# Decoder layer on one core: a seven-product matrix scheme with three accumulators, another order of outputs, residual by token halves

## The chip, the core and the metric

The kernel runs on one core of one Trainium2 chip. The metric is the device time of one execution in microseconds (us). Before the change three runs gave a median of 2959.45 us (2957.71 to 2963.02).

## What is computed

One layer of a hybrid decoder for a prompt of 2048 tokens of width 1024 and a sample group of 8 rows. All products are float32 and carried out to nearly float32 precision. Cut to what matters:

```
h = rmsnorm(x, g_pre);  proj = h @ w_in            # 1024 x 10248
q, k: short causal conv and SiLU;  v, o, z_a, u, v_b, z_b, gate_a, gate_b
branch A: mLSTM (4 heads x 256, chunks of 128), head norm, * sigmoid(o) * silu(z_a), @ w_pa
branch B: u * (tril(W_s) layernorm(v_b) + b) * silu(z_b), @ w_pb
merged = sigmoid(gate_a) * A + sigmoid(gate_b) * B
x = x + rmsnorm(merged @ w_out, g_post)
x = x + sigmoid(x @ w_ple_gate) * rmsnorm(p @ w_ple, g_ple)
```

The sample rows go through the same layer with a stored state for each row and head (`state_C`, 256 x 256), which is read, scaled, updated, used and written back.

## The kernel before

The prompt is worked through in four passes `p` of 512 tokens. In pass 1 (`SP`) the 8 sample rows ride along: four columns more in each token half (260 in place of 256), and their own small steps. A pass is a list of 28 units (`PASS`, L53): `v`, `qk`, `og`, `gg` for each of four heads, then `ub` 0 to 3, then `pa`, `pb`, `wo` and `wg`, two of each. A unit multiplies a 1024 x 512 piece of weights with 512 tokens. It is done as a 2 x 2 block product with seven block products in place of eight (the Winograd form of Strassen's scheme): weights A11 to A22 with the sums S1 to S4, tokens B11 to B22 with the sums T1 to T4. Outputs are named (i, l): i is the column block of the weights, l the token half. `ORDER` (L58) lists the products with their accumulators in PSUM; `LATE` (L60) is another order for the unit `wo 0`, whose tokens come out of the unit `pb 1` just before it.

A block product is 24 matmuls: four slices of the contraction, two output blocks, and three terms each, because every operand is split into a high and a low part (`whi`, `wlo` for weights, `rhi`, `rlo` for tokens). ScalarE (ACT) makes the high part (`copy`, L124) and VectorE (DVE) the low part (`sub_hi`, L129); in pass 0 each fourth weight split has its low part on GpSimd (POOL). `Stream` feeds the weights: it loads some five to seven products ahead into 13 buffers. In pass 0 it also makes the sums S1 to S4 on DVE (L136, L139) and stores them, with S1, S2 and S4 already split (`CUT_KEPT`, L63). The stores and loads all go through one queue, issued by SyncE (SP, lines L117 and L120).

`run_unit` runs the products. After some of them ACT copies an accumulator to SBUF (`snap`: tiles `s` and `u`), and DVE adds such a copy to another accumulator when an output is finished and handed to `consumer`. Before the change: `a` takes A11, S2, S3 and A22, `b` takes A12, `c` takes S1, `d` takes S4. `s` is `a` after A11, `u` is `a` after S2. After S1 DVE adds `c` to `u` in place (L139, tile `u<-acc,u`); that sum completes (0,1). After S3 a second copy `u` of `a` completes (1,1) together with `c`. The outputs come in the order (0,0), (1,1), (0,1), (1,0), and (1,0) needs no add. PSUM has eight banks, shared with all small products (`acc` and `smp`); an accumulator takes one, in most units of pass 1 two.

Smaller work is written as generators: `qa`, `qb` and `qc` hold them, and `pump` in `run_unit` advances them by one step at set places between the matmuls, `drain` finishes a queue. `ahead` is a generator that is advanced once after each product. The order that the engines see is set by a planner at compile time: it goes by the order of the program and by its own estimate of when operands and buffers are free. Buffers come from pools: `t2` (`tmp`, ten), `t1` (`tiny`, eight), `p4` (`piece`, ten).

Around the change:
- `sample_head(h)` is queued on `qb` one head late (L1055, L1058). It loads two rows' state and `vb` (`load_state`), scales and updates them (`update_state`, L1116) and multiplies them (L1180).
- `b_norm` queues `sample_b` on `qc` and drains `qc` at once; `sample_b` normalises the sample's `xs` (L1229, L1230) and transposes it (L405).
- `merge` runs `pa` and `pb`. `ready` cuts the merged tokens into B11, B22, T1 to T4 and B21 for `wo`, partly between the products of `pb 1`, partly (`ready(True)`) between those of `wo 0`.
- `out_phase` runs `wo 0` and `wo 1`, scales the output by `g_post` (L1529, L1534), and takes the row scale `ors` from the sums of squares (`rms_tail`). Then the steps of `ple` (p @ w_ple in four column blocks, L1477, scaled by a `gple` loaded in the step, L1481) alternate with `residual(kh, l)`, which loads `xr` and does x + scale * output (L1549), and `turn`, which transposes the result (L1557) into `xblk`. `cut` and `sub` make B11 to T4 of the unit `wg 0` from it.

## Time and profile before

| | |
|---|---|
| runs | 2957.71, 2959.45, 2963.02 us |
| profiled execution, own time | 2958.16 us |
| its span, first to last instruction | 2956.4 us |
| mean granted TensorE clock | 0.966 |
| instructions | 56209 |
| moved by DMA | 770.38 MB, mean 261 GB/s |

PE is TensorE, DVE is VectorE, ACT is ScalarE, POOL is GpSimd, SP is the queue that issues the DMAs. L124 is a line of the kernel; helpers such as `copy` have one line for all their uses, so the tile names (out<-in) tell the uses apart, without buffer numbers. Times of an event are us from the start of the span. A matmul's end is modelled, so it is the starts that show the pace. The clock is a share of 2.4 GHz: 1.00 or 0.50.

### The profile page before, as it was taken

The numbers are of one execution on the slowest core, as the hardware profiler recorded it, in microseconds if no ns is written. First come the engines' busy times: TensorE is split into PE (matmuls) and PEld (weight loads), VectorE is DVE, ScalarE is ACT, GpSimd is POOL, SyncE is SP. The second block draws the span as 40 slices with busy tenths as digits, with TensorE's granted clock in tenths as the row PEclk, the third lists the DMA queues.
The fourth block names the chain that finished last, engine by engine and source line by source line (L and its number), as shares of the span: only waits on it lengthen the run. The fifth ranks groups of instructions, "written<-read, shape, count | busy, mean of one in ns | idle before, by whom it ended". The sixth has DMA issues, their size and how long they took to land. (4 is left out here: it accounts for less than half of the span.)

```text
span 2956.4 us, 56209 instructions
## 1 busy us (share of the span) xinstructions
PE 2724.2 (92%) x21835; PEld 2652.2 (90%) x21835; DVE 2216.6 (75%) x3641; ACT 1569.1 (53%) x2704; POOL 480.3 (16%) x549
## 2 busy tenths in 40 slices
PE   6999899787799999998988999999998999999897
PEld 6898889787789998888988999999998999999897
DVE  7898988788787766767768766765778766765776
ACT  4655656444646645544456555554456555554454
POOL 3333333223220001001012100001021100001010
PEclk9999999898899999999999999999999999999999
DMA  5566657775686887868867877778887877788886
GB/s 213 211 244 258 240 222 263 269 271 217 234 289 232 276 266 258 288 224 309 316 210 245 280 254 257 255 269 292 319 282 258 282 257 260 255 271 282 301 292 202
DMA packets 268628, 770.38 MB, mean 261 GB/s; under 512 B 30065, under 2 KB 89337, under 8 KB 268354
## 3 DMA queue, kind: packets, MB, share of 16 engines
q1 hardware_dynamic: 268362, 766.79, 74.3%
q8 instruction: 172, 2.82, 0.4%
q14 instruction: 94, 0.77, 0.1%
HBM read 595.29 MB, written 171.53 MB: 259 GB/s over the span
## 5 line engine op out<-in xcount | busy, mean ns | idle before, releaser
L487 PE MATMUL acc<-rhi,wlo 128*128 128x256 f32 (+1 forms) x4480 | 1276.9, 286 | 59.5 <-DVE wlo L129 46.6
L487 PE MATMUL acc<-rhi,whi 128*128 128x256 f32 (+1 forms) x4480 | 1291.7, 289 | 38.4 <-ACT whi L124 24.6
L487 PE MATMUL acc<-rlo,whi 128*128 128x256 f32 (+1 forms) x4480 | 1276.1, 285 | 0.0
L487 PEld LDWEIGHTS acc<-rhi,wlo 128*128 128x128 f32 x4480 | 859.9, 193 | 70.3 <-DVE wlo L129 55.5
L487 PEld LDWEIGHTS acc<-rhi,whi 128*128 128x128 f32 x4480 | 861.3, 192 | 51.1 <-ACT whi L124 28.8
L487 PEld LDWEIGHTS acc<-rlo,whi 128*128 128x128 f32 x4480 | 860.9, 192 | 0.4 <-issue 0.4
L129 DVE TENSOR_TENSOR wlo<-wraw,whi 128x1024 fp32r<-128x1024 f32 (+1 forms) x461 | 590.8, 1286 | 168.8 <-PE acc L487 66.3
L124 ACT ACTIVATE whi<-wraw 128x1024 fp32r<-128x1024 f32 (+1 forms) x503 | 527.3, 1053 | 295.5 <-PE acc L487 88.8
L484 PE MATMUL acc<-whi,rhi 128*128 128x256 f32 (+1 forms) x1792 | 518.9, 291 | 19.4 <-ACT rhi L124 7.1
L484 PE MATMUL acc<-wlo,rhi 128*128 128x256 f32 (+1 forms) x1792 | 512.1, 288 | 13.8 <-DVE wlo L129 11.8
L484 PE MATMUL acc<-whi,rlo 128*128 128x256 f32 (+1 forms) x1792 | 512.1, 287 | 7.6 <-DVE rlo L129 7.6
L484 PEld LDWEIGHTS acc<-whi,rhi 128*128 128x128 f32 x1792 | 347.7, 194 | 25.7 <-ACT whi L124 8.5
L484 PEld LDWEIGHTS acc<-wlo,rhi 128*128 128x128 f32 x1792 | 345.9, 194 | 16.9 <-DVE wlo L129 14.2
L484 PEld LDWEIGHTS acc<-whi,rlo 128*128 128x128 f32 x1792 | 347.5, 194 | 8.5 <-DVE rlo L129 8.3
L124 ACT ACTIVATE u<-acc 128x512 f32<-128x512 f32 (+1 forms) x272 | 140.7, 520 | 354.3 <-PE acc L487 287.9
L129 POOL TENSOR_TENSOR wlo<-wraw,whi 128x512 fp32r<-128x512 f32 x84 | 146.0, 1758 | 227.8 <-ACT whi L124 203.4
L139 DVE TENSOR_TENSOR u<-acc,u 128x512 f32<-128x512 f32 (+1 forms) x136 | 80.4, 592 | 80.5 <-PE acc L487 52.6
L124 ACT ACTIVATE s<-acc 128x512 f32<-128x512 f32 (+1 forms) x136 | 70.1, 518 | 99.7 <-PE acc L487 77.1
L786 POOL TENSOR_TENSOR so<-so,sz 128x512 f32<-128x512 f32 (+1 forms) x32 | 45.9, 1433 | 317.5 <-DVE sz L783 314.9
L1281 POOL TENSOR_TENSOR yb<-yb,ub 128x512 f32<-128x512 f32 (+1 forms) x32 | 46.5, 1459 | 296.4 <-DVE ub L1279 95.7
L241 POOL TENSOR_SCALAR aab<-au 128x2 f32<-128x2 f32 x32 | 7.7, 239 | 509.5 <-DVE au L879 508.5
L865 DVE SCALAR_TENSOR_TENSOR cext<-cext,fst,smp 128x258 f32<-128x258 f32 x128 | 60.3, 477 | 37.7 <-PE smp L802 37.5
(367 smaller groups left out, 3972.4 us busy)
## 6 DMA issues: line engine op xcount, KB each, us to landing
wraw<-in_w_main SPq DMA_DIRECT2D x351, 512.0 KB
xh<-xh SPq DMA_DIRECT2D x32, 512.0 KB
sg<-sgm SPq DMA_DIRECT2D x24, 512.0 KB
gsig<-sg SPq DMA_DIRECT2D x24, 512.0 KB
x<-in_x_prompt SPq DMA_DIRECT2D x16, 512.0 KB
ya<-ya SPq DMA_DIRECT2D x32, 256.0 KB
pg<-pg SPq DMA_DIRECT2D x32, 256.0 KB
xr<-in_x_prompt SPq DMA_DIRECT2D x32, 256.0 KB
```

What stands on the lines that cost most here:

```text
L124: S.activation(out, in_, AF.Copy)
L129: eng.tensor_tensor(lo, full, hi.bitcast(F32), op=ALU.subtract)
L139: (eng or V).tensor_tensor(out, a, b, op=ALU.add)
L241: G.tensor_scalar(out, ms, EPS, None, op0=ALU.add)
L484: T.matmul(outs[s], x[:, kt, s * P:(s + 1) * P], wt[:, kt, :], start=first, stop=last, skip_group_check=not opens)
L487: T.matmul(outs[s], wt[:, kt, s * P:(s + 1) * P], x[:, kt, :], start=first, stop=last, skip_group_check=not opens)
L786: G.tensor_tensor(so[:, s], so[:, s], sz[:, s], op=ALU.mult)
L865: V.scalar_tensor_tensor(cext[:, h, kt, :], cext[:, h, kt, :], gt.fst[:, h, self.c:self.c + 1], p3, op0=ALU.mult, op1=ALU.add)
L1281: G.tensor_tensor(y[:, :, l, :], y[:, :, l, :], ub[:, :, l, :], op=ALU.mult)
```

## The change

- `ORDER` becomes A11 (a), A12 (b), S2 (a), S3 (c), S1 (a), A22 (c), S4 (a): three accumulators. `u` after S2 is kept as it is, `u` after S3 is a copy of `c`. (1,1) is `a` after S1 plus the copy of S3, (1,0) is `c` after A22 plus the copy of S2, (0,1) is `a` after S4 with no add. So there are three adds per unit, and the outputs come as (0,0), (1,1), (1,0), (0,1).
- `LATE` becomes A11, S3, S2, A12, S1, A22, S4. The sums of its weights are made one product earlier, and A12 isn't loaded early any more. The order in which T1, T3, T4 and B22 are cut follows.
- In `pb` the column blocks of the weights and the token halves are swapped, so that (1,1) of the merged tokens is finished first, and (1,0) last, as before.
- The sample's state is loaded after the product of the two rows before, three steps ahead of its scaling; updates, convolution and normalisation get more steps between them; `sample_head(h)` is queued with its own head, and `sample_b` isn't drained at once.
- In `out_phase` the row scale is made by token halves, the first half within `wo 1`; `gple` (all four) and the `xr` of token half 0 are loaded during `wo 1`, those of half 1 right after a residual step has freed the buffers; residual, turn and cut follow by token halves.

```diff
-    UNITS["pb", _j] = ("w_pb", 256 * _j, 512 + 256 * _j)
+    UNITS["pb", _j] = ("w_pb", 512 + 256 * _j, 256 * _j)
...
-ORDER = [("A11", "B11", "a", True), ("A12", "B21", "b", True), ("S2", "T2", "a", False), ("S1", "T1", "c", True),
-         ("S3", "T3", "a", False), ("S4", "B22", "d", True), ("A22", "T4", "a", False)]
-LATE = [ORDER[i] for i in (0, 5, 2, 3, 4, 1, 6)]
+ORDER = [("A11", "B11", "a", True), ("A12", "B21", "b", True), ("S2", "T2", "a", False), ("S3", "T3", "c", True),
+         ("S1", "T1", "a", False), ("A22", "T4", "c", False), ("S4", "B22", "a", False)]
+LATE = [ORDER[i] for i in (0, 3, 2, 1, 4, 5, 6)]
...
-            first = "S4" if order(u) is LATE else "S2"
+            first = "S3" if order(u) is LATE else "S2"
...
         sub(b12, b22, b12)
+        cut("T3", b12)
+        yield
+        sub(b21, b21, t2)
         cut("T1", b11)
         yield
-        sub(b21, b21, t2)
-        cut("T3", b12)
+        cut("T4", b21)
         yield
         cut("B22", b22)
-        yield
-        cut("T4", b21)
         yield
...
             elif wn == "S2":
                 u2 = snap("u2", "a")
+            elif wn == "S3":
+                u3 = snap("u3", "c")
             elif wn == "S1":
-                for sel, ps in accs["c"][1]:
-                    add(u2[:, sel, :], ps, u2[:, sel, :])
-                x2 = u2
-            elif wn == "S3":
-                u3 = snap("u3", "a")
-                consumer(1, 1, Out(accs["c"][1], u3, w))
+                consumer(1, 1, Out(accs["a"][1], u3, w))
             elif wn == "A22":
-                consumer(1, 0, Out(accs["a"][1], None, w))
+                consumer(1, 0, Out(accs["c"][1], u2, w))
                 if so is not None:
                     consumer("sample", sos, None)
-            if x2 and "d" in accs:
-                consumer(0, 1, Out(accs["d"][1], x2, w))
-                x2 = None
+            else:
+                consumer(0, 1, Out(accs["a"][1], None, w))
...
-            if p == SP and h:
-                qb.append(sample_head(h - 1, st, A.gt, A.yad))
+            if p == SP:
+                qb.append(sample_head(h, st, A.gt, A.yad))
             gg_unit(A, h)
-        if p == SP:
-            qb.append(sample_head(H - 1, st, A.gt, A.yad))
...
-        update_state(0)
+        yield
+        yield from update_state(0)
         yield from rest(3)
         hps = smp([NS, DH])
         for i in range(4):
-            if i + 1 < 4:
-                load_state(i + 1)
             for b in range(2):
...
             if i < 3:
-                yield
-                update_state(i + 1)
+                load_state(i + 1)
                 yield from rest(3)
+                yield from update_state(i + 1)
+                yield from rest(2)
...
             qc.append(sample_b(A.xs, st, mv, rs, A.sm))
-            drain(qc)
...
-            run_unit(p, ("pa", j), ra, False, done, ahead=from_dram(rb, A.ybd) if j else None)
+            run_unit(p, ("pa", j), ra, False, done, ahead=from_dram(rb, [d[::-1] for d in A.ybd]) if j else None)
...
             yield
+            cut("B22", at(0, 1, 1), 0)
+            yield
+            cut("B22", at(1, 1, 1), 1)
+            yield
             cut("B11", at(0, 0, 0), 0)
             yield
             cut("B11", at(1, 0, 0), 1)
-            yield
-            cut("B22", at(0, 1, 1), 0)
-            yield
             subs(0)
-            cut("B22", at(1, 1, 1), 1)
             yield
             cuts(0)
             subs(1)
...
             def done(i, l, o):
+                i, l = 1 - i, 1 - l
                 m, g = ma[j][i][:, :, l, :], sg[i][:, :, l, :]
...
+        def fetch_x(kh, l):
+            for nq in (2 * kh, 2 * kh + 1):
+                x = xrs[nq, l] = tmp([P, 2, 256], "xr")
+                load(x, rows_of("x_prompt", 256 * nq)[:, 2 * l:2 * l + 2, :])
+
+        def fetch_ahead():
+            yield
+            for n in range(4):
+                gams.append(tiny([P, 256], "gple"))
+                load(gams[n], I["g_ple"][0, 256 * n:256 * n + 256].partition_broadcast(P))
+            yield
+            yield
+            fetch_x(0, 0)
+            yield
+            yield
+            fetch_x(1, 0)
...
+                if d == 1 and (i, l) == (1, 0):
+                    rms_part(ss, rs, 0, 2)
+
+            run_unit(p, ("wo", d), rm, True, done, slhs, fetch_ahead() if d else late)
         drain(qc)
-        rms_tail(ss, rs, n)
+        rms_part(ss, rs, 2, NC)
...
         next(embed)
         next(embed)
+        residual(0, 0)
+        fetch_x(0, 1)
+        next(embed)
+        residual(1, 0)
+        fetch_x(1, 1)
+        turn(0, 0)
+        cut("B11", xblk[0, 0])
...
         next(embed)
+        turn(1, 0)
+        residual(0, 1)
+        cut("B21", xblk[1, 0])
...
         next(embed, None)
+        residual(1, 1)
+        turn(0, 1)
...
         sub(xblk[0, 1], xblk[1, 1], xblk[0, 1])
-        cut("T1", xblk[0, 0])
+        cut("T3", xblk[0, 1])
         rms_tail(ss2, rs2, n)
         sub(xblk[1, 0], xblk[1, 0], t2)
-        cut("T3", xblk[0, 1])
+        cut("T1", xblk[0, 0])
+        cut("T4", xblk[1, 0])
         cut("B22", xblk[1, 1])
-        cut("T4", xblk[1, 0])
```

## Rows read from the trace of the kernel before

**Rows 1.** The page's first part: busy us, share of the span, instructions.

```profile
PE 2724.2 (92%) x21835; PEld 2652.2 (90%) x21835; DVE 2216.6 (75%) x3641; ACT 1569.1 (53%) x2704; POOL 480.3 (16%) x549
```

**Rows 2.** Stretches: length, busy (instructions) by engine, clock, DMA share, GB/s.

```profile
2421.30:2462.00 40.70, 40.70 (x346) 40.70 (x345) 29.89 (x45) 25.89 (x40) 2.68 (x4) 1.00 0.75 258
...
742.00:791.10 49.10, 32.73 (x227) 30.81 (x226) 36.27 (x48) 27.24 (x71) 11.65 (x10) 0.79 0.73 250
1526.10:1578.50 52.40, 37.91 (x278) 36.30 (x277) 35.66 (x66) 28.32 (x84) 8.71 (x12) 0.84 0.59 188
2205.20:2249.00 43.80, 33.40 (x227) 31.18 (x225) 29.22 (x42) 23.96 (x65) 7.10 (x8) 0.84 0.75 244
2879.50:2918.80 39.30, 30.53 (x226) 28.17 (x225) 26.54 (x40) 21.43 (x60) 6.90 (x6) 0.91 0.74 239
...
907.60:1384.80 477.20, 453.36 (x3587) 423.16 (x3586) 325.13 (x755) 248.12 (x471) 43.85 (x86) 0.99 0.79 264
1683.30:2077.60 394.30, 390.48 (x3283) 389.25 (x3282) 257.18 (x445) 211.74 (x358) 31.59 (x65) 1.00 0.78 267
...
18.20:575.20 557.00, 492.17 (x3842) 479.54 (x3841) 484.69 (x666) 310.02 (x471) 178.07 (x152) 0.94 0.65 240
1619.30:2077.60 458.30, 453.29 (x3807) 451.31 (x3806) 312.17 (x558) 247.79 (x410) 43.90 (x73) 1.00 0.78 267
...
683.70:723.80 40.10, 29.81 (x194) 28.75 (x193) 29.75 (x40) 20.09 (x37) 13.68 (x7) 0.83 0.47 170
...
2217.20:2220.60 3.40, 3.31 (x16) 3.11 (x16) 1.52 (x4) 0.00 (x0) 0.00 (x0) 0.50 0.90 295
```

**Rows 3.** Waits of PE over the span: us in total, times, longest.

```profile
PE smp L1557 <- DVE xq L1549: 32.2, 14, 9.5
...
PE smp L1180 <- DVE cs L1116: 12.8, 7, 6.1
...
PE acc L487 <- ACT u L124: 10.0, 14, 2.0
...
PE smp L405 <- DVE xos L1573: 8.0, 2, 5.1
```

**Rows 4.** DVE in order of time, tail of pass 2: start, us, what.

```profile
2214.32 1.29 DVE L1481 TENSOR_TENSOR pg<-acc,gple 128x512 f32<-128x512 f32 x2 [3.19 <-DMA gple<-in_g_ple]
...
2220.01 0.88 DVE L1549 SCALAR_TENSOR_TENSOR xq<-xq,ors,xr 128x256 f32<-128x256 f32 x2 [1.88 <-DMA xr<-in_x_prompt]
...
2240.90 1.22 DVE L136 TENSOR_TENSOR xblk<-xblk,t 128x1024 f32<-128x1024 f32 x1
2242.03 1.22 DVE L129 TENSOR_TENSOR rlo<-t,rhi 128x1024 fp32r<-128x1024 f32 x1
```

**Rows 5.** SP's issues in order of time, tail of pass 2.

```profile
2211.63 0.43 SPq L117 DMA_DIRECT2D xr<-in_x_prompt  x1
```

**Rows 6.** PE in order of time, tail of pass 2.

```profile
2217.29 1.08 PE L1557 MATMUL smp<-ident,xq 128*128 128x128 f32 x4 [3.30 <-DVE xq L1549]
```

**Rows 7.** DVE in order of time, pass 1, behind the unit `gg 3`.

```profile
1254.80 1.67 DVE L1116 SCALAR_TENSOR_TENSOR cs<-vb,kd,cs 128x256 f32<-128x256 f32 x4 [4.28 <-DMA vb<-svd]
```

**Rows 8.** The add of the product S1, in groups of DVE: busy, mean ns, idle before.

```profile
L139 DVE TENSOR_TENSOR u<-acc,u 128x512 f32<-128x512 f32 (+1 forms) x136 | 80.4, 592 | 80.5 <-PE acc L487 52.6 <-PE acc L484 20.8 <-ACT rhi L124 4.2
```

**Rows 9.** DVE in order of time, pass 2, from `pb 1` to `wo 0`.

```profile
2165.82 0.68 DVE L139 TENSOR_TENSOR mt<-acc,u 128x512 f32<-128x512 f32 x1
...
2173.04 0.68 DVE L129 TENSOR_TENSOR rlo<-t,rhi 128x512 fp32r<-128x512 f32 x1
2173.64 2.49 DVE L129 TENSOR_TENSOR rlo<-gsig,rhi 128x512 fp32r<-128x512 f32 x4
```

**Rows 10.** ACT in order of time: `pb 1` of pass 2, `og 1` of pass 3.

```profile
2161.09 0.60 ACT L124 ACTIVATE u<-acc 128x512 f32<-128x512 f32 x1 [1.76 <-PE acc L487]
...
2435.79 0.60 ACT L124 ACTIVATE u<-acc 128x512 f32<-128x512 f32 x1 [1.67 <-PE acc L487]
```

**Rows 11.** DVE in order of time, `og 1` of pass 3.

```profile
2436.88 0.68 DVE L139 TENSOR_TENSOR sz<-acc,u 128x512 f32<-128x512 f32 x1
```

More of the change, by code (lines that the diff above doesn't have):

```diff
@@ L284, in load @@
             else:
-                late = order(u) is LATE
-                for m in {"A11": ("A11", "A21", "A22") + ("A12",) * late, "A12": ("A12",) * (not late)}.get(n, ()):
+                for m in {"A11": ("A11", "A21", "A22"), "A12": ("A12",)}.get(n, ()):
                     self.fetch((p, u, m), given(m))
@@ L300, in sum @@
             at = self.raw
-            a11, a12, a21, a22 = (at[p, u, m] for m in RAW)
+            a11, a21, a22 = (at[p, u, m] for m in ("A11", "A21", "A22"))
             if n == first:
@@ L310, in sum @@
             if n == "S4":
-                s4 = self.tile(u, "wsum") if first == "S4" else a12
-                sub(s4, a12, at[p, u, "S2"])
+                s4 = at[p, u, "A12"]
+                sub(s4, s4, at[p, u, "S2"])
                 self.keep(u, "S4", s4)
@@ L1112, in update_state @@
             for b in range(2):
+                if b:
+                    yield
                 bb = 2 * i + b
@@ L1129, in sample_head @@
             for j in range(1, 4):
+                if j == 2:
+                    yield
                 x = st[:, ks, :, j] if j < 3 else sqk[:, ks, :]
@@ L1155, in sample_head @@
         V.tensor_copy(qm.rearrange("p t a b -> p t (a b)")[:, :, 0::NS + 1], qs)
-        yield from rest(4)
+        yield from rest(3)
         cps = smp([NS, 2, P])
@@ L1226, in sample_b @@
             load(bl, I["b_lnv"][0, cs].partition_broadcast(NS))
+            yield from rest(2)
             x = xs[i]
@@ L1231, in sample_b @@
             store(O["chunk_v_sample"][0, :, 0, cs], x)
-        yield
+        yield from rest(2)
         for i in range(2):
@@ L1411, in merge, with rms_part, rms_tail @@
         return rm, lhs[0], ready(True)
-    def rms_tail(ss, rs, n):
+    def rms_part(ss, rs, c0, c1):
         ms = small([P, NC + 1], "oms")
-        V.tensor_reduce(ms[:, 0:NC], ss[:, 0:NC, :], axis=AX.X, op=ALU.add)
-        pow_rstd(rs[:, 0:NC], ms[:, 0:NC])
+        V.tensor_reduce(ms[:, c0:c1], ss[:, c0:c1, :], axis=AX.X, op=ALU.add)
+        pow_rstd(rs[:, c0:c1], ms[:, c0:c1])
+    def rms_tail(ss, rs, n, c0=0):
+        rms_part(ss, rs, c0, NC)
         if n > NC:
+            ms = small([P, NC + 1], "oms")
             V.tensor_reduce(ms[0:NS, NC:], ss[0:NS, NC:, :], axis=AX.X, op=ALU.add)
@@ L1461, in ple_weights, with ple @@
             yield
-    def ple(p, box, pgd, ss2, pgs):
+    def ple(p, box, pgd, ss2, pgs, gams):
         for n in range(4):
@@ L1467, in ple @@
             hi, lo = (x[:, :, (n % 2) * 256:(n % 2 + 1) * 256] for x in box.w[n // 2])
-            gam = tiny([P, 256], "gple")
-            load(gam, I["g_ple"][0, cs].partition_broadcast(P))
+            gam = gams[n]
             for l in range(2):
@@ L1508, in out_phase @@
         qc.append(ple_weights(pbox))
+        gams, xrs = [], {}
+        def fetch_x(kh, l):
[3 more added lines that the diff above has]
+        def fetch_ahead():
+            yield
+            for n in range(4):
+                gams.append(tiny([P, 256], "gple"))
+                load(gams[n], I["g_ple"][0, 256 * n:256 * n + 256].partition_broadcast(P))
+            yield
+            yield
+            fetch_x(0, 0)
+            yield
+            yield
+            fetch_x(1, 0)
         for d in range(2):
@@ L1534, in done @@
                     G.tensor_tensor(xq[nq][:, sl, :], xq[nq][:, sl, :], gb, op=ALU.mult)
-            run_unit(p, ("wo", d), rm, True, done, slhs, None if d else late)
+                if d == 1 and (i, l) == (1, 0):
+                    rms_part(ss, rs, 0, 2)
+            run_unit(p, ("wo", d), rm, True, done, slhs, fetch_ahead() if d else late)
         drain(qc)
-        rms_tail(ss, rs, n)
-        embed = ple(p, pbox, pgd, ss2, pgs)
+        rms_part(ss, rs, 2, NC)
+        if p == SP:
+            ms = small([P, NC + 1], "oms")
+            V.tensor_reduce(ms[0:NS, NC:], ss[0:NS, NC:, :], axis=AX.X, op=ALU.add)
+            pow_rstd(rs[0:NS, NC:], ms[0:NS, NC:])
+        embed = ple(p, pbox, pgd, ss2, pgs, gams)
         xblk = {}
@@ L1573, in out_phase @@
                 V.scalar_tensor_tensor(xs[i], xs[i], rs[0:NS, NC:], r, op0=ALU.mult, op1=ALU.add)
-        residual(0, 0)
         next(embed)
+        turn(1, 0)
+        residual(0, 1)
+        cut("B21", xblk[1, 0])
         if p == SP:
@@ L1579, in out_phase @@
                 samp_T(xst[:, 4 * i:4 * i + 4, :], xs[i], 4)
-        residual(1, 0)
-        turn(0, 0)
-        cut("B11", xblk[0, 0])
-        next(embed)
-        residual(0, 1)
-        turn(1, 0)
-        cut("B21", xblk[1, 0])
         next(embed, None)
+        residual(1, 1)
+        turn(0, 1)
         if p == SP:
@@ L1590, in out_phase @@
                 slhs2 = samp_part(lhs, xst, part)
-        residual(1, 1)
-        turn(0, 1)
         sub(xblk[0, 0], xblk[0, 1], xblk[0, 0])
@@ L1608, in out_phase @@
             pg = {}
-            for i, l in ((0, 0), (1, 1), (0, 1), (1, 0)):
+            for i, l in ((0, 0), (1, 1), (1, 0), (0, 1)):
                 pg[i, l] = tmp([P, 2, 256], "pgl")
@@ L1623, in done @@
                     return
-                nq = 2 * d + i
+                nq, last = 2 * d + i, i != l
                 sg = tmp([P, 2, 256], "osg")
@@ L1635, in done @@
                 V.tensor_tensor(xq[nq][:, 2 * l:2 * l + 2, :], xq[nq][:, 2 * l:2 * l + 2, :], sg, op=ALU.add)
-                if (i, l) in ((0, 1), (1, 0)):
+                if last:
                     store(O["y_prompt"][0, p * TP:(p + 1) * TP, 256 * nq:256 * nq + 256].rearrange(
```

9 lines of the change are left out of this document (3 added, 6 removed).

## The prediction

> **What bounds the kernel now.** I read the page first, then a table of stretches, then the PE waits, then the timelines of the stretches that lose most. The page gives PE 92% busy, DVE 75% and ACT 53% [rows 1], so the question is what PE loses, and a busy share does not tell that: matmul ends are modelled. I use the pitch instead. In 40.7 us without a wait there are 346 matmuls, 117.6 ns each [rows 2]. 21835 matmuls [rows 1] at that pitch are 2568 us, so about 390 us of the 2956.4 us span are lost, and a stretch's loss is its length less its count times 0.1176.
>
> By stretch [rows 2]: the four changes from the output product to the gate product (last product of `wo 1` to third product of `wg 0`, here "tails") lose 22.4, 19.7, 17.1 and 12.7 us, together 72. (First: 49.1 - 227 x 0.1176.) The middle of pass 1, which carries the sample rows, loses 477.2 - 421.8 = 55.4; the same stretch of pass 2 loses 394.3 - 386.1 = 8.2, so the sample rows cost 47. The front of pass 0 loses 105, that of pass 2 only 11; those 95 us belong to the weight sums and splits that only pass 0 makes. The unit `wo 0` loses 17.3 in pass 0.
>
> The list of PE waits names the causes [rows 3]: transposes L1557 wait for the residual L1549 (32.2 us), sample transposes for `xos` (8.0), the sample's state product L1180 for `cs` (12.8). In the tail of pass 2 the cause is late loads: DVE stands 3.19 us until `gple` lands and later 1.88 until `xr` lands [rows 4]; the first `xr` is issued only at 2211.63 [rows 5], and PE is idle 3.30 us before its first transpose [rows 6]. Afterwards the granted clock is 0.50, that is 1.2 GHz, and 16 matmuls take 3.4 us where 29 would fit [rows 2].
>
> **The change, part by part.**
>
> *Tails.* `gple` and half of `xr` are loaded during `wo 1`, tokens of half 0 get their scale after the third consumer, and only then the second `xr` half is fetched. Nothing is computed more, except one small reduction and two POOL operations per pass, off the path. Eight issues of about 0.43 us [rows 5] move earlier on SP, past weight loads that wait for free buffers anyway. What is late next is the DVE chain to T2, which the third product of `wg 0` needs: eight `pg` and the last scaled output at 0.64 (half of the 1.29 for two [rows 4]), sixteen residual steps at 0.44 (0.88 for two), two low parts and two subtractions at 1.13 (the last two of [rows 4] start that far apart), then a high part of ACT, taken like a low part, and T2's low part: 5.8 + 7.0 + 4.5 + 2.3 = 19.6 us, with one weight split 20.7. PE has 96 embedding matmuls, 32 transposes and two products of 24 to do meanwhile: 176 x 0.1176 = 20.7. So DVE is just hidden, with nothing to spare; in pass 0 the weight sums come on top and in pass 1 the sample rows. I leave a loss of 5 us in passes 2 and 3, 8 in pass 1, 11 in pass 0, together 29: gain 43. Far end: 3.5 left in each, gain 58. Near end: the named waits alone go in part, gain 25.
>
> *Sample rows.* The drain of `sample_b` behind the last gate unit goes, each state is fetched three steps before it is scaled, not one, and updates are halved into two steps. Today the last head waits 4.28 us for `vb` [rows 7], PE 6.1 us for the state [rows 3], then twice for `xs`. The named waits of L1180 in that kernel are 12.8; with `xs`, the split weights behind them and the half clock they make some 29 of the 47. The rest is small matmuls that stay. I take 18; ends 5 (waits move to another step) and 29.
>
> *Seven products in another order.* One DVE add per unit goes: 136 instructions, 80.4 us [rows 8], 592 ns each. In passes 1 to 3 DVE is not late, and this is worth 0. In pass 0 there are 22 units ahead of the merge, 13 us of DVE at most; the waits there are chains (sum, high part, low part), so I take 5, ends 0 and 13. The weight S4 is summed one product later and used one product later: 0.
>
> *The boundary to `wo 0`.* Its order becomes A11, S3, S2, A12, S1, A22, S4. T3 is wanted by the second product where before T2 was wanted by the third, and B21 by the fourth instead of the sixth. `cuts` still makes T2, T1, T3 in that order. In pass 2 the third output of `pb 1` is read by DVE at 2165.82; T2's last low part starts at 2173.04, the four others follow from 2173.64 [rows 9], so T3's is done near 2174.9. The end of product five of `pb 1` is where ACT is released to copy `u`, just before 2161.09 [rows 10], so 2160.9; two more products of 24 x 0.1176 = 2.82 end it at 2166.5, and the second half of S3 times T3 would start at 2166.5 + 2.82 + 1.41 = 2170.8. That is up to 4.1 us of waiting; if PE takes half of S2 meanwhile, 2.7, and if the planner cuts T3 first, less. I take 2.5 per pass, +10; ends 0 and +16. Swapping the token halves of `pb` (so that B22 and B11 come first) costs nothing: the same operations, the same loads.
>
> *A new wait.* Before, accumulator `a` was freed by ACT copies and (1,1) and (0,1) had banks of their own. Now S4, the last product, adds into `a`, and must wait until DVE has read `a` for output (1,1) after S1. A22 lies between, 2.82 us. Behind the waiting matmul stands everything on PE. In a unit of pass 3 ACT copies `u` from 2435.79, when product five has ended, and DVE starts the add of (1,1) at 2436.88, done at 2437.56 [rows 10, 11]: 1.8 us after the product's end, 1.0 to spare. Now it has no ACT copy to wait for. I take +4 in all for the few units with loads in the way; ends 0 and +15. That PE does wait for such reads is seen: 10.0 us in 14 places for ACT's `u` [rows 3]. In the Trainium skill, "PSUM — Partial Sum Buffer", section Terms, says that TensorE may not write a bank while VectorE reads it; this speaks against putting a DVE read between two products of one bank, and by it the wait is as long as DVE is late, with 0 in the sum for a DVE in time. The row of 1.0 us to spare decides for the small value.
>
> **The sum.** -43 - 18 - 5 + 10 + 4 = -52. The profiled execution took 2958.2 us (span 2956.4 and 1.8 around it), 1.3 below the median of 2959.45. So 2906, as a median **2907 us**. All near ends: -25 - 5 + 16 + 0 + 15 = +1, 2960. All far ends: -58 - 29 - 13 = -100, 2859.
>
> **The rivals.**
>
> *DVE or ACT becomes the bound of the tail.* For it: the sum above leaves no cover, and ACT has much to do there too (sixteen sums of squares, eight `xblk` copies). Against: DVE is busy 29.2 of 43.8 us there [rows 2], so a third of it is waiting that goes. Then half of the gain of 43 stays away: 2928.
>
> *The loads don't come early.* The planner gives `xr` and `gple` buffers when it thinks them free; four `xr` tiles, three copies of accumulators and the `pwr` tiles share ten buffers, in pass 1 with two sample tiles more. Then the change doesn't do what it says: the tail gains 5, 2945. Against it: with one `pwr` tile at a time passes 2 and 3 need eight of the ten.
>
> *S4 waits for DVE in every unit.* This is the slower one. If the add of (1,1) comes behind two weight splits and a convolution step (2 x 1.13 and an estimated 0.7, beside its own 0.68), it ends 3.7 us after S1, 0.9 too late; 112 units x 0.9 = 100 us, 3005. It decides from 2.82 - 0.68 = 2.1 us of DVE lag; 0.5 us per unit eats the whole gain, 2960. For it: DVE is at 75% [rows 1], in the front of pass 0 at 87% [rows 2]. Against: in the row of pass 3 the add waited for ACT's copy, which is now older by a product.
>
> *All far ends.* The small loads, the half clock and the sample waits all vanish: 2859.
>
> **How the numbers follow.** Forecast (2885 to 2930): 0.54. Tail bound by DVE: 0.15. Loads not early: 0.08. Far ends: 0.05. S4 waits: 0.18, of which 0.06 end within 0.2% and 0.12 above it. The range 2862 to 2957 leaves out the 0.12 and about half of the far ends. 0.2% is 5.9 us, about what a measurement of this kernel tells from no change. Faster 0.82, same 0.06, slower 0.12.
>
> **What would show it.** Right: waits of L1557 for `xq` below 8 us in the whole run, no DVE wait for `gple`, tails at 32 us with clock near 1; L1180 waiting under 4 us; 136 fewer `u<-acc,u` adds; a PE wait for `rlo` of 1 to 4 us early in `wo 0`. Wrong: PE waits that name a DVE add such as `so`, `raw` or `mt`; DVE idle for `xr` in the tail as before; tails over 38 us with DVE full; new waits for `whi` or `wlo` in passes 2 and 3.

## The result, and the profile after

The changed kernel took 2915.39 us (median of four runs, 2913.75 to 2918.81) against 2958.58 before: a ratio of 0.9853, 95% interval 0.9836 to 0.987, or 43.5 us less (38 to 48). The forecast was 2907, the range 2862 to 2957. The sign and the two main terms (tails and sample rows) were right, the size was missed by 8 us, and the terms on the new order came out otherwise than forecast. In what follows a ratio to the kernel before is turned into us with 29.6 us for one per cent.

The page of after, its first part, as in [rows 1]:

```profile
PE 2705.6 (93%) x21835; PEld 2634.8 (90%) x21835; DVE 2139.5 (73%) x3513; ACT 1542.8 (53%) x2668; POOL 494.0 (17%) x557
```

Stretches of after: length, busy (instructions) by PE, PEld, DVE, ACT and POOL, clock, DMA share, GB/s. The first four are the tails of passes 0 to 3, the fifth is the middle of pass 1 with the sample rows, the sixth that stretch of pass 2, the last two `wo 0` of passes 2 and 3 (as in [rows 2]):

```profile
742.10:779.80 37.70, 26.57 (x188) 25.15 (x188) 32.76 (x48) 25.37 (x65) 19.32 (x10) 0.86 0.69 230
1494.20:1536.60 42.40, 33.89 (x274) 33.21 (x273) 35.84 (x68) 28.97 (x86) 9.85 (x13) 0.92 0.67 219
2167.70:2202.80 35.10, 28.55 (x222) 27.51 (x223) 30.94 (x49) 27.28 (x73) 8.56 (x12) 0.95 0.82 295
2844.30:2874.20 29.90, 26.59 (x223) 25.75 (x222) 26.33 (x41) 22.03 (x62) 6.70 (x8) 1.00 0.84 289
...
899.50:1355.30 455.80, 447.95 (x3579) 420.46 (x3578) 312.18 (x720) 242.11 (x463) 44.04 (x85) 1.00 0.83 276
1643.20:2035.60 392.40, 388.92 (x3283) 386.92 (x3282) 249.91 (x426) 208.02 (x350) 43.74 (x65) 1.00 0.79 267
...
2125.40:2149.70 24.30, 22.16 (x170) 21.55 (x169) 19.07 (x28) 13.12 (x27) 3.63 (x2) 0.93 0.75 254
2803.70:2827.00 23.30, 20.80 (x171) 19.98 (x171) 18.86 (x28) 11.94 (x23) 2.91 (x2) 1.00 0.77 259
```

Each loss is length less count times 0.1176, as in the prediction. The tails lose 15.6, 10.2, 9.0 and 3.7, together 38.5 where they lost 72: 33.5 us gained, and the clock rises with it. The middle of pass 1 loses 34.9 where it lost 55.4: 20.5 gained. `wo 0` of passes 2 and 3 loses 4.3 and 3.2 where it lost 0.4 and 1.3. Over all four `wo 0` the sum is -0.9, since pass 0 gained 5.1 there, and the front of pass 0 gained 1.5. The span fell by 44.4 (2956.4 to 2912.0), so the rest of the kernel lost about 12.

PE's waits in after: us in total, times, longest (as in [rows 3]; L1584 is the old L1557 and L1178 the old L1180):

```profile
PE smp L1584 <- DVE xq L1576: 15.3, 7, 4.2
...
PE acc L485 <- DVE sz L139: 6.0, 3, 2.0
PE acc L485 <- DVE mt L139: 5.6, 6, 2.7
...
PE acc L485 <- DVE zb L139: 2.3, 2, 1.2
PE acc L485 <- DVE raw L139: 2.1, 3, 0.7
PE smp L1178 <- DVE cs L1110: 2.0, 3, 1.0
...
PE acc L482 <- DVE xq L139: 1.4, 2, 0.9
```

The wait for the residual has halved and that for `cs` has nearly gone. Five rows are new: PE waits 17.4 us, in 16 places, for DVE to read an accumulator. No row of DVE waits for `gple` any more. So of the signs that the prediction named, three of the right kind came (`gple`, `cs` under 4, 136 adds `u<-acc,u` fewer) and three came in part or not at all (`xq` below 8, tails at 32 us, `rlo` in `wo 0`). Two of the wrong kind came as well: waits that name `raw` and `mt`, and new waits for `whi` in passes 2 and 3.

### The profile page after: what moved, and what is told of

Its sections match the earlier page's. It is cut to its first block, busy times and chain, and to the rows that moved or that the text cites. A ratio compares the mean times of both kernels' runs of the same rounds, so it can differ in the third digit from the quotient of the medians.

```text
span 2912.0 us, 56022 instructions
## 1 busy us (share of the span) xinstructions
PE 2705.6 (93%) x21835; PEld 2634.8 (90%) x21835; DVE 2139.5 (73%) x3513; ACT 1542.8 (53%) x2668; POOL 494.0 (17%) x557
## 3 DMA queue, kind: packets, MB, share of 16 engines
q8 instruction: 172, 2.82, 0.4%
## 4 chain that ended last, share of the span: by engine, by line
PE 58%; DVE 12%; DMA 5%; issue 3%; ACT 3%; SPq 1%; POOL 0%; DVEq 0%; ACTq 0%; POOLq 0%
PE acc L485 36%; PE acc L482 14%; DVE wlo L129 3%; PE smp L796 3%; DVE rlo L129 2%; DVE wraw L136 1%; PE smp L491 1%; DMA blk<-ya 1%; PE smp L816 1%; PE smp L1178 1%; ACT whi L124 1%; DMA vb<-svd 1%; PE acc L1480 1%; SPq L117 1%; PE smp L1255 0%
## 5 line engine op out<-in xcount | busy, mean ns | idle before, releaser
L485 PE MATMUL acc<-rhi,whi 128*128 128x256 f32 (+1 forms) x4480 | 1290.0, 288 | 58.1 <-ACT whi L124 25.9
L485 PE MATMUL acc<-rhi,wlo 128*128 128x256 f32 (+1 forms) x4480 | 1273.9, 285 | 47.2 <-DVE wlo L129 40.2
L482 PEld LDWEIGHTS acc<-wlo,rhi 128*128 128x128 f32 x1792 | 343.1, 192 | 15.3 <-DVE wlo L129 14.3
L129 POOL TENSOR_TENSOR wlo<-wraw,whi 128x512 fp32r<-128x512 f32 (+1 forms) x84 | 146.0, 1758 | 314.5 <-ACT whi L124 254.8
L780 POOL TENSOR_TENSOR so<-so,sz 128x512 f32<-128x512 f32 (+1 forms) x32 | 56.4, 1763 | 287.0 <-ACT so L764 191.6
L1280 POOL TENSOR_TENSOR yb<-yb,ub 128x512 f32<-128x512 f32 (+1 forms) x32 | 53.5, 1681 | 290.2 <-DVE ub L1278 159.2
L859 DVE SCALAR_TENSOR_TENSOR cext<-cext,fst,smp 128x258 f32<-128x258 f32 x128 | 60.4, 478 | 35.8 <-PE smp L796 35.6
L129 DVE TENSOR_TENSOR rlo<-blk,rhi 128x1024 fp32r<-128x1024 f32 (+1 forms) x48 | 58.9, 1236 | 34.7 <-ACT rhi L124 34.6
```

Source lines behind the costliest of these rows:

```text
L129: eng.tensor_tensor(lo, full, hi.bitcast(F32), op=ALU.subtract)
L482: T.matmul(outs[s], x[:, kt, s * P:(s + 1) * P], wt[:, kt, :], start=first, stop=last, skip_group_check=not opens)
L485: T.matmul(outs[s], wt[:, kt, s * P:(s + 1) * P], x[:, kt, :], start=first, stop=last, skip_group_check=not opens)
L780: G.tensor_tensor(so[:, s], so[:, s], sz[:, s], op=ALU.mult)
L859: V.scalar_tensor_tensor(cext[:, h, kt, :], cext[:, h, kt, :], gt.fst[:, h, self.c:self.c + 1], p3, op0=ALU.mult, op1=ALU.add)
L1280: G.tensor_tensor(y[:, :, l, :], y[:, :, l, :], ub[:, :, l, :], op=ALU.mult)
```

## The experiments

The table by pass below is used by several of these runs.

### The three parts alone, and two of them together

`e_order` is the kernel before with the hunks on `ORDER`, `LATE`, `pb`, the weight sums and the cuts only. `e_tail` has those of `out_phase` and `ple` only, `e_sample` those of the sample rows only. Example lines of each:

```diff
# e_order
+ORDER = [("A11", "B11", "a", True), ("A12", "B21", "b", True), ("S2", "T2", "a", False), ("S3", "T3", "c", True),
+         ("S1", "T1", "a", False), ("A22", "T4", "c", False), ("S4", "B22", "a", False)]
# e_tail
+            run_unit(p, ("wo", d), rm, True, done, slhs, fetch_ahead() if d else late)
# e_sample
+                load_state(i + 1)
                 yield from rest(3)
+                yield from update_state(i + 1)
```

> The kernel before with only the other order of the seven products (three accumulators, three adds, the cuts of the token sums and the halves of pb that go with it); sample rows and tails as before. Theory (parts add up, and the order is about worth nothing): the stretches of the changed kernel show wo 0 at -1, the front of pass 0 at -1.5 and about +12 elsewhere, among it new PE waits for DVE reads such as sz, mt and zb of about 17 us; so this run is 0 to 15 us slower than before, 2958 to 2973. Rival A (as predicted, one add less is worth 5 in pass 0 and the boundary costs 10, S4 waits 4): +9, 2967, with the 10 at wo 0. Rival B (the order carries part of the gain, through less DVE work and fewer PSUM banks): 10 or more us faster, below 2949.

Measured: 1.0021 (1.001 to 1.0033), 6 us slower (3 to 10).

> The kernel before with only the early loads of gple and xr, the row scale by token halves and the residual by halves; order of the products and sample rows as before. With the old order the output (1,0) is the last one, so the scale of half 0 comes after the last output here, not after the third. Theory (parts add up; the early loads are most of it): the four tails gain about 25 to 33 us, 2926 to 2934. Rival (the scale must be there one product early, so the new order is what makes the tails shorter): the tails gain 15 us or less, 2944 or more, and e_order and e_tail together are far less than the whole.

Measured: 0.9868 (0.9849 to 0.9886), 39 us faster (34 to 45), although the scale of half 0 comes after the last output here.

> The kernel before with only the sample rows in smaller steps (state fetched earlier, halved updates, no drain behind the last gate unit). Theory: the middle of pass 1 loses 55.4 before and 34.9 after, so this alone gives -15 to -20 us, 2939 to 2944, with the waits of the state product for cs gone. Rival (the sample stretch gained by the new order, which needs fewer PSUM banks where an accumulator takes two of the eight): the waits only move, -5 us or less, 2954 or more.

Measured: 0.9909 (0.989 to 0.9928), 27 us faster (21 to 33).

The new order carries none of the gain, so both rivals of that kind fall. Which of the sample edits gains is not separated: in `e_sample` DVE still waits 14.3 us for `vb` in all (15.7 before), while PE's wait for `cs` falls to 2.5 us. The three add up to -60, the whole is -43.5. The next run asks where the difference is.

> The kernel before with the tails and the sample steps of the change, and with the old order of the seven products. Alone these two parts gave 0.9868 and 0.9909 of the time before, the new order 1.0021. Theory (the new order only costs, and the other two add up): 0.978, 2892 to 2902, some 15 us better than the changed kernel. Rival (the 12 us that are missing between the sum of the three parts and the whole are lost between tails and sample steps, both of which lengthen DVE's queue in pass 1): 2905 to 2912.

Measured: 2902.25 us, 0.9802 (0.9781 to 0.9823), 59 us faster (52 to 65). Tails and sample rows lose at most a little to each other; the new order on top of them costs 15 us (the two intervals leave 4 to 26). Where it costs them is in a table by pass: the same columns as above, passes 0 to 3 of each kernel.

Before:

```profile
18.20:835.40 817.20, 700.42 (x5371) 678.88 (x5370) 706.77 (x925) 442.69 (x699) 261.39 (x210) 0.93 0.66 243
835.40:1619.30 783.90, 732.83 (x5818) 696.55 (x5817) 563.45 (x1180) 409.72 (x786) 80.11 (x128) 0.97 0.78 263
1619.30:2286.00 666.70, 644.03 (x5326) 637.41 (x5325) 476.46 (x771) 359.09 (x612) 70.56 (x104) 0.98 0.80 274
2286.00:2956.40 670.40, 639.77 (x5296) 632.61 (x5294) 463.67 (x754) 344.07 (x584) 61.58 (x87) 0.99 0.77 266
```

After:

```profile
17.50:825.70 808.20, 695.31 (x5370) 671.01 (x5370) 680.02 (x898) 437.57 (x693) 264.71 (x211) 0.94 0.68 244
825.70:1576.30 750.60, 723.75 (x5819) 692.14 (x5818) 544.32 (x1136) 401.12 (x777) 82.28 (x132) 0.99 0.82 276
1576.30:2239.40 663.10, 640.06 (x5326) 633.10 (x5325) 462.19 (x744) 354.45 (x604) 72.13 (x103) 0.99 0.81 276
2239.40:2912.00 672.60, 639.41 (x5296) 631.82 (x5294) 446.80 (x724) 336.21 (x573) 68.27 (x88) 0.99 0.78 266
```

Tails and sample rows with the old order (`e_tail_sample`):

```profile
17.80:823.80 806.00, 694.93 (x5371) 675.12 (x5370) 703.11 (x926) 442.58 (x699) 265.60 (x213) 0.94 0.67 246
823.80:1579.70 755.90, 724.31 (x5818) 690.71 (x5818) 556.85 (x1182) 404.28 (x784) 86.95 (x130) 0.99 0.81 273
1579.70:2235.00 655.30, 639.67 (x5327) 633.66 (x5326) 473.97 (x771) 359.12 (x614) 64.25 (x103) 0.99 0.81 279
2235.00:2896.00 661.00, 636.73 (x5296) 630.69 (x5294) 463.18 (x755) 343.53 (x584) 61.52 (x89) 0.99 0.78 270
```

The losses of the passes are 185.6, 99.7, 40.4, 47.6 before, 176.7, 66.3, 36.8, 49.8 after, and 174.4, 71.7, 28.8, 38.2 with the old order. So the new order, put on top of the two other parts, costs 2 in pass 0, gains 5 in pass 1, and costs 8 and 12 in passes 2 and 3, where DVE has the most room. Differences of a few us in one pass are not firm: `e_t3first`, whose kernel differs from after only at the end of `pb 1`, loses 6 more in pass 1 and 5 less in pass 3. The 8 and 12 are `wo 0` for 6 of these 20, `qk 0` for another 5 (2.7 and 2.8, at the sixth product, where PE waits 1.03 us for the high part of a weight); the rest is spread over `ub 1`, `pa 0`, `pb 0` and `pb 1`, and is not settled unit by unit.

### Tails: which part of the edit gains, and what is left

```diff
# e_late_loads: the loads at their use again, the halves kept
-            run_unit(p, ("wo", d), rm, True, done, slhs, fetch_ahead() if d else late)
+            run_unit(p, ("wo", d), rm, True, done, slhs, None if d else late)
...
         def residual(kh, l):
+            fetch_x(kh, l)
# e_late_scale: the scale for all chunks after the last output
-                if d == 1 and (i, l) == (1, 0):
-                    rms_part(ss, rs, 0, 2)
...
-        rms_part(ss, rs, 2, NC)
+        rms_part(ss, rs, 0, NC)
# e_gpost_dve: the last g_post product by DVE
-                    G.tensor_tensor(xq[nq][:, sl, :], xq[nq][:, sl, :], gb, op=ALU.mult)
+                    (V if d and i else G).tensor_tensor(xq[nq][:, sl, :], xq[nq][:, sl, :], gb, op=ALU.mult)
```

> The changed kernel, but gple is loaded in its embedding step and xr in its residual step, as before; order by token halves and early row scale are kept. Theory (the early loads are nearly the whole gain of the tails, 33 us by their stretches): 2938 to 2950. Rival (half of it is the order by token halves, which lets transposes and cuts of half 0 start before half 1 is scaled): 2925 to 2933.

Measured: 2949.63 us, 0.9972 (0.9962 to 0.9981), 35 us slower than after. DVE waits for both loads again, 35.6 us in 26 places (us in total, times, longest):

```profile
DVE xq L1578 <- DMA xr<-in_x_prompt: 23.4, 18, 2.7
DVE pg L1485 <- DMA gple<-in_g_ple: 12.2, 8, 3.1
```

The four tails lose 71.9 in this run, as much as before. So nothing of the gain is left without the early loads, and the order by halves is worth nothing by itself. Whether the loads would give as much without that order, no run tells.

> The changed kernel with the row scale made only after the last output, for all four chunks at once; the early loads and the order by token halves are kept. Theory (the early loads are the gain of the tails; with the tails part alone, where the scale also comes last, the tails lost as little as in after): within 4 us of after, 2911 to 2919. Rival (the early scale starts the residual 2.8 us earlier in each pass): 8 to 12 us slower, 2923 to 2927.

Measured: 2912.94 us, 0.9838 (0.9818 to 0.9857): no difference from after.

> The changed kernel, but the last g_post product before the row scale, output (1,0) of wo 1, is done by DVE (0.68 us) and not by POOL (1.29 us), where it stands ahead of the two POOL operations that make the scale. Theory (the prediction called the POOL operations off the path; in the tail of pass 2 of after the first residual starts when POOL ends the scale, 1.29 us of which are that product, and PE then waits 1.82 us): the first residual comes 1.3 us earlier in each pass, 3 to 5 us in all, 2910 to 2913. Rival (DVE's own work sets the tail, so a piece moved to DVE costs what it frees): no change within 2 us, or slower by up to 3.

Measured: 2914.29 us, 0.9842 (0.9821 to 0.9863): no difference from after either; by their stretches the four tails lose 36.5 and 34.8 in these two runs in place of 38.5, and the kernels' times do not show even that. The early scale and the place of that product are not what is left in the tails. What is left shows beside `e_tail`, whose tails lose 7.3, 10.3, 6.2 and 4.1, together 27.9 (columns as above):

```profile
744.80:778.20 33.40, 28.81 (x222) 27.51 (x222) 31.92 (x46) 24.34 (x67) 12.01 (x12) 0.95 0.80 277
1511.70:1554.20 42.50, 34.74 (x274) 33.66 (x273) 35.01 (x67) 28.03 (x83) 10.82 (x14) 0.88 0.65 220
2183.90:2216.70 32.80, 29.10 (x226) 27.80 (x225) 28.61 (x44) 23.88 (x67) 7.10 (x10) 0.95 0.89 295
2848.10:2878.70 30.60, 27.32 (x225) 26.14 (x225) 27.85 (x44) 22.23 (x63) 6.92 (x8) 1.00 0.84 287
```

Most of the 10.6 us between 27.9 and 38.5 are in pass 0, but there the two stretches are not alike: that of `e_tail` begins just behind a wait of PE, and 222 matmuls lie in it where after has 188, since after does 34 of the embedding's matmuls earlier. The wait, in `e_tail`:

```profile
744.77 0.58 PE L484 MATMUL acc<-whi,rhi 128*128 128x256 f32 x1 [5.03 <-ACT u L124]
```

From the end of `wo 0` to the same third product of `wg 0` the counts agree. Pass 0 of before, after and `e_tail`:

```profile
723.80:791.10 67.30, 50.49 (x371) 48.02 (x370) 50.50 (x62) 37.21 (x89) 16.71 (x14) 0.85 0.74 252
717.20:779.80 62.60, 48.99 (x370) 46.89 (x370) 48.53 (x64) 36.87 (x88) 25.87 (x15) 0.92 0.72 243
720.80:778.20 57.40, 47.03 (x370) 44.99 (x368) 48.53 (x62) 35.37 (x86) 17.85 (x16) 0.97 0.79 279
```

These lose 23.7, 19.1 and 13.9. In stretches that begin so in all four passes, before loses 75.6, after 42.6 and `e_tail` 37.2. `e_tail` thus gains 38.4, which agrees with the 39 of its time, after gains 33.0, and the 5 us between them are those of pass 0 (in passes 1 to 3 the two differ by 0, 2 and -2). POOL there, in order of time in after, then DVE and PE (start, us, what):

```profile
743.10 4.44 POOL L129 TENSOR_TENSOR wlo<-wraw,whi 128x512 fp32r<-128x512 f32 x2 [3.40 <-ACT whi L124]
747.50 1.26 POOL L1556 TENSOR_TENSOR xq<-xq,gpost 128x512 f32<-128x512 f32 x1
748.84 0.22 POOL L241 TENSOR_SCALAR ors<-oms 128x2 f32<-128x2 f32 x1
749.15 0.71 POOL L242 TENSOR_TENSOR ors<-ors,mhalf 128x2 f32<-128x2 f32 x1
...
749.89 0.48 DVE L1576 SCALAR_TENSOR_TENSOR xq<-xq,ors,xr 128x256 f32<-128x256 f32 x1 [3.48 <-POOL ors L242]
...
750.43 0.44 PE L1584 MATMUL smp<-ident,xq 128*128 128x128 f32 x2 [4.16 <-DVE xq L1576]
```

The two POOL operations that make the scale stand behind a weight split of 4.44 us on POOL; DVE waits 3.48 us for them and PE 4.16 us for DVE. This wait is no work of the new order, though: before and in `e_tail` the same two halves of a split stand on POOL ahead of the scale, and the scale ends later still (in `e_tail` the first residual starts at 753.75). What differs is that after has fewer embedding matmuls left for PE to do meanwhile; that this costs the 5 us is likely, and no run shows it by itself. In pass 2 the weight S3 of `wg 0`, which comes unsplit and is now the fourth product instead of the fifth, has its low part in DVE's queue between the token sums, and PE waits for it (PE in order of time):

```profile
2198.54 0.50 PE L482 MATMUL acc<-wlo,rhi 128*128 128x256 f32 x1 [1.89 <-DVE wlo L129]
```

This matmul is one of four of S3 that the planner has put ahead of the 24 of the third product, S2.

### What S4's wait costs, and what an add is worth

```diff
# e_s4own
+            if wn == "S4" and packed:
+                an, opens = "d", True
...
+                x2 = snap("x2", "a") if packed else None
...
-                consumer(0, 1, Out(accs["a"][1], None, w))
+                consumer(0, 1, Out(accs[an][1], x2, w))
# e_add_c_pass0; e_add_a_pass0 has the same in the line of consumer(1, 1)
-                    add(dst(sel), ps[..., c], self.extra[:, sel, c])
+                    for _ in range(1 + self.more):
+                        add(dst(sel), ps[..., c], self.extra[:, sel, c])
...
-                consumer(1, 0, Out(accs["c"][1], u2, w))
+                consumer(1, 0, Out(accs["c"][1], u2, w, p == 0))
```

> The changed kernel, but in every unit with 256 columns the product S4 gets an accumulator of its own, ACT copies `a` after S1 and DVE adds that copy to S4's accumulator: one ACT copy and one DVE add more per unit, and S4 waits for no DVE read. Theory (the order's loss is S4 waiting for DVE's read of `a`, 17.1 us in 14 places of the trace of after): these 17 us go, the extra add gives back at most 5 in pass 0: 8 to 15 us faster than after, 2900 to 2907. Rival (the waits that name DVE only stand where PE would wait for split weights anyway, so the loss is from the cuts and the stalls behind them): within 4 us of after or slower by the added work, 2911 to 2925.

Measured: 2929.0 us, 0.9898 (0.988 to 0.9916), 13 us slower than after. The waits that name a DVE read are gone but for 0.7 us of `mt`; the waits for split weights are up instead. PE's waits in `e_s4own`:

```profile
PE acc L487 <- DVE wlo L129: 50.3, 42, 5.1
PE acc L487 <- ACT whi L124: 27.7, 18, 5.8
PE acc L487 <- POOL wlo L129: 15.4, 9, 3.1
```

In after these rows are 40.2, 25.9 and 6.4. By pass the loss moved from 176.7 to 190.9 in pass 0, by +6 in pass 1, and by -7 in passes 2 and 3 together. In after the named waits on DVE reads are 12.4 us in pass 0, 0.2 in pass 1, and 4.8 in passes 2 and 3 together. So where there is next to no such wait (pass 1) the added work only cost; in passes 2 and 3 the gain is of the size of the wait, if near what two executions differ by; and in pass 0 one ACT copy and one DVE add per unit cost more than the wait.

> The changed kernel, but in pass 0 the add of output (1,0), which reads accumulator `c` after A22, is done twice (the second writes the same values): 28 DVE adds of 0.6 to 0.7 us more, 17 to 19 us of DVE time, with nothing on PE that waits for `c`. It prices one DVE add per unit in pass 0. Theory (with S4 in an accumulator of its own, pass 0 lost 14.6 us more although 12 us of S4's waits went; so an add there costs nearly its own time): +11 to +18, 2926 to 2933. Rival (as predicted, the waits in pass 0 are chains of sum, high part and low part, and an add is worth a quarter microsecond): +3 to +7, 2918 to 2922.

Measured: 2933.1 us, 0.9915 (0.9901 to 0.993), 18 us slower than after; pass 0 loses 190.6 in place of 176.7, the others stay. That is 13.9 us for 28 adds more, 0.5 us each, near the 0.6 us that one takes. Pass 0 of this run:

```profile
17.30:839.50 822.20, 705.64 (x5371) 680.93 (x5370) 696.78 (x929) 436.52 (x693) 268.15 (x211) 0.93 0.67 240
```

> The same, but the add that is done twice is that of output (1,1), which reads accumulator `a` after S1 and for which S4 waits. The order of PE's instructions has S4's first two matmuls moved ahead of all but two of A22's in 7 units of pass 0 in the changed kernel and in 8 with the add of (1,0) doubled, here in 2 only. Theory (where S4's matmuls stand early in A22 the wait costs 0.7 to 2.7 us, so without them S4 waits less, and the doubled add costs what one of (1,0) costs or less): equal to e_add_c_pass0 within 5 us or up to 6 us faster. Rival (S4 waits for each DVE read, as the prediction's slow rival had it; each of 28 units waits up to 0.68 us longer): 8 to 19 us slower than e_add_c_pass0.

Measured: 2931.12 us, 0.9901 (0.9888 to 0.9914), 14 us slower than after; not different from the run before. S4 does not wait for each read in full, so the slow rival of the prediction falls. In `og` of pass 0, where it does wait, the wait for `sz` grows from 6.0 us in after to 11.9.

Where it does wait is in the order of PE's instructions. In `qk 1` of pass 0 the compiled order of after is (accumulator <- tokens, weights; `acc_2044` is `c`, `acc_1925` is `a`):

```
1072 L485 MATMUL acc_2044<-rhi_264,whi_2045 128x256 [waits Activation_49]
1073 L485 MATMUL acc_2044<-rlo_265,whi_2045 128x256
1074 L485 MATMUL acc_1925<-rhi_268,whi_2086 128x256 [waits DVE_49,Activation_49]
1075 L485 MATMUL acc_1925<-rlo_269,whi_2086 128x256
```

The planner has put two matmuls of S4 ahead of the 22 others of A22, apparently because it took A22's low part to be late. The cover is then two matmuls, not 24. It does so in seven units of pass 0 (`qk` 1 to 3, `pa` and `wo`). In time, DVE first:

```profile
183.28 0.69 DVE L139 TENSOR_TENSOR raw<-acc,u 128x512 f32<-128x512 f32 x1 [5.05 <-PE acc L485]
...
184.12 0.35 PE L485 MATMUL acc<-rhi,whi 128*128 128x256 f32 x1 [0.71 <-DVE raw L139]
```

DVE had stood idle for 5.05 us and read at once, and PE still waits 0.71. In `og` 1 to 3 of pass 0 it is DVE that is late: S1's last matmul starts at 205.49 and A22's first at 205.60, so S1 has ended by about 205.8, and DVE comes to the add 5.3 us later, behind convolution steps and a weight split (POOL's line first):

```profile
202.75 5.13 POOL L129 TENSOR_TENSOR wlo<-wraw,whi 128x512 fp32r<-128x512 f32 x2 [10.47 <-ACT u L124]
...
204.94 3.50 DVE L708 SCALAR_TENSOR_TENSOR k<-raw,vecs,k 128x512 f32<-128x512 f32 x2
...
209.95 1.21 DVE L129 TENSOR_TENSOR wlo<-wraw,whi 128x1024 fp32r<-128x1024 f32 x1
211.09 0.68 DVE L139 TENSOR_TENSOR sz<-acc,u 128x512 f32<-128x512 f32 x1
...
211.82 0.38 PE L485 MATMUL acc<-rhi,whi 128*128 128x256 f32 x1 [1.99 <-DVE sz L139]
```

Two of these convolution steps take 3.50 us together, where one takes 0.74 in the median, and a weight split on POOL runs beside them. It is so in all three units (3.50, 3.49 and 3.52). The 2 us too much are as long as S4's wait; no run tests whether they are its cause.

### T3 first, and a mixed order

```diff
# e_t3first
             def cuts(j):
+                cut("T3", at(j, 0, 1), j)
                 cut("T2", t2[j], j)
                 cut("T1", at(j, 0, 0), j)
-                cut("T3", at(j, 0, 1), j)
# e_mixed: e_tail_sample, with the new order in some units of pass 0
+def order(unit, p=1):
+    if p == 0 and unit[0] in ("v", "og", "gg", "ub"):
+        return THREE
```

> The changed kernel with T3 cut ahead of T2 and T1 at the end of pb 1. Theory (the second product of wo 0 waits for T3, which is cut last): in passes 2 and 3 wo 0 loses 4.3 and 3.2 us against 0.4 and 1.3 before; with T3 first 2 to 3 us of each pass go, 4 to 10 us in all, 2906 to 2911. Rival (ACT and DVE are the bound there, so that T2, needed by the third product, is then late in its place): no change within 3 us, 2912 to 2918, and the wait names the high part of T2.

Measured: 2914.72 us, 0.9845 (0.9823 to 0.9866): not different from after. `wo 0` of passes 2 and 3 loses 2.7 and 2.6 in place of 4.3 and 3.2. The wait for the high part of T3 (`rhi`; the prediction had named `rlo`) is gone, but at the same matmul of `wo 0` (the 14th of the second product) PE now waits for `s`, ACT's copy of the first accumulator, which stands in ACT's queue behind the cuts. Pass 2, first after, then this run:

```profile
2132.22 0.87 PE L482 MATMUL acc<-whi,rhi 128*128 128x256 f32 x2 [1.49 <-ACT rhi L124]
```

```profile
2138.39 0.39 PE L482 MATMUL acc<-whi,rhi 128*128 128x256 f32 x1 [2.21 <-ACT s L124]
```

So T3's wait was real, and with T3 first ACT is the bound there, as the rival had it, though by its copy `s` and not by T2's high part. What is left of the gain, some 2 us in the two units, is below what a run can tell.

> The kernel with the tails and the sample steps of the change and the old order of products (2902.25), but with the new order in the units v, og, gg and ub of pass 0, where S4 was not moved ahead in PE's order; qk, pa, pb, wo and wg and all of passes 1 to 3 keep the old order. Theory (one DVE add less is worth 0.5 us per unit in pass 0, and S4's wait does not eat it in these units): 16 units x 0.5 = 8 us faster, 2891 to 2898. Rival (the split weights behind it only wait elsewhere, as they did between ub 1, ub 2 and ub 3 when the order was changed alone): within 3 us, 2899 to 2905.

Measured: 2899.88 us, 0.9796 (0.9783 to 0.981), 60 us faster than before and not different from `e_tail_sample`. So the gain of 8 us did not come, and the time is the rival's. But the theory had taken it that S4 does not wait in these units, and the trace shows that it does: 6.0 us in `og` 1 to 3. An add less at 0.5 us in 16 units, with this wait, would leave 2 us, which is what was measured and less than can be told from none. What an add less is worth by itself this run does not decide. PE in `e_mixed` (total, times, longest):

```profile
PE acc L494 <- DVE sz L145: 6.0, 3, 2.0
```

These two are the fastest kernels of the study, some 15 us below the changed one.

## Why the prediction was right, and where its terms were off

**The reading of the profile** held: the tails and the sample rows were where PE lost time that could be had, and late loads were the cause in the tails. Taking the early loads away again cost 35 us and brought the loss of the tails back to what it was.

**Tails, forecast -43, measured -33.5.** For the edit by itself the 43 lies within the interval: `e_tail` is 39 us faster (34 to 45), 38.4 by stretches. Together with the new order 33 are left. I had costed the parts one by one: "96 embedding matmuls" to do meanwhile failed in pass 0, where with the new order 34 of them are done before the tail, and the count of "one weight split" has S3's low part beside it in DVE's queue in pass 2. That these two make the 5 us is likely and not shown. The step "two POOL operations per pass, off the path" failed as well: in pass 0 they stand behind a weight split on POOL, with the old order and with the new, and in after DVE and PE wait for them. The waits of L1584 are 15.3 us and not below 8, and only the tail of pass 3 has 30 us and clock 1.00. The rival that DVE becomes the bound of the tail is partly true in pass 1: 42.4 us with DVE busy for 35.8. The early scale, which I had counted among the causes, is worth nothing that can be measured.

**Sample rows, forecast -18, measured -20.5** by the stretch and -27 (21 to 33) alone. L1178 waits 2.0 us for `cs`, where I had asked for under 4.

**One add less, forecast -5.** An add more costs 0.5 us in pass 0, by the doubled add, so 28 of them 14. If an add less gave back as much, the term was too small, and the step that failed is "the waits there are chains": any DVE work in that pass would delay the low parts that PE waits for, though DVE is busy for 84% of it (680.0 of 808.2). That it does give back as much is not shown: pass 0 gained 5.2 with the order alone (185.6 to 180.4), and `e_mixed` leaves it open. The count was off as well: a pass has 20 units ahead of `pa` and 28 in all, not 22, so 11.8 us of DVE work ahead of the merge and 16.6 in all.

**S4's wait, forecast +4, the named waits are 17.4.** The step "A22 lies between, 2.82 us" failed. I read the cover from the order of the program, and the planner moves S4's first matmuls ahead; and my row of 1.0 us to spare came from pass 3, while in `og` of pass 0 the lag is 5.3 us, beyond the 2.1 that I had named as the point that decides. The rule from the Trainium skill, "PSUM — Partial Sum Buffer", section Terms, that TensorE may not write a bank while VectorE reads it, is one that the kernel keeps, and the trace agrees with it: the matmul at 184.12 starts 0.15 us after the add's end. No run lets the two overlap. The 0 for a DVE in time did not hold, since in `qk` DVE read at once and PE waited all the same.

**Both errors would nearly cancel in pass 0**, if the -14 holds: the named waits there are 12.4 (2.1 in `qk`, 6.0 in `og`, the rest in `pa` and `wo 0`), against -5.2 that pass 0 gained when the order was changed alone. That is an argument; no run takes the two apart.

**Boundary to `wo 0`, forecast +10, measured -0.9.** In passes 2 and 3 it was right in place and size (+3.9 and +1.9 against 2.5 each), by the wait for T3 that I had named. In pass 0 `wo 0` gained 5.1 and in pass 1 1.6, which I had not foreseen. That the order also costs elsewhere in passes 2 and 3, I had not in the sum.

The net of the three terms on the order was forecast at +9 and measured alone at +6 (3 to 10): right as a sum of terms of which none was shown right, and so by luck. Together with the other parts it costs about 15. By stretches, the 8 us by which the forecast was too low are 9.5 less gained in the tails, 3.5 less at the front of pass 0 and 8 more lost in the rest (12 in place of 4), against 11 better at `wo 0` and 2.5 better in the sample rows.

## What to carry to other kernels

Load small operands one stage ahead of a boundary before rearranging anything else there: without the early loads, nothing of what the tails had gained was left. Where a planner orders the instructions, read the cover of a new wait from its order, not from the program's. A part that saves work can still cost when it moves other work into a stretch with no slack, so measure a change's parts alone and together.

## What the runs showed of the hardware

POOL's half of a weight split (128x512) took 1.27 us at its shortest and 1.46 in the median (84 of them in after), but 2.22 us each at 743.10 in after, where the DVE sum `wraw` of two SBUF tiles (128x1024) ran beside it and took 2.19 us in place of 1.22. Both took longer side by side here, and in the `og` units above two DVE steps took 3.50 us beside two halves of a split on POOL that took 5.13. The DVE sum `wsum` at 742.98, which adds two SBUF tiles as well but started 0.12 us before POOL's split, took its usual 1.22. "GPSIMD Engine Reference" of the Trainium skill, section 1. Specifications, says that GpSimd shares its SBUF interfaces with VectorE and contends with DVE instructions that have two SBUF inputs; the trace agrees for the sum that ran second. No run here isolates it.
